# Feed-forward gate and up products as 2x2 block products with seven multiplications

## The chip, the cores and the metric

The kernel runs on one core of one Trainium2 chip. The metric is the device time of one execution in microseconds (us). A core has five engines that run side by side, each taking its own instructions in program order: TensorE (PE in the profile) multiplies matrices into PSUM banks of 128 x 512 floats, VectorE (DVE), ScalarE (ACT) and GpSimd (POOL) work elementwise, and SyncE (SP) issues most of the loads. Engines wait for one another by semaphores; DMA transfers run beside all of them.

## What is computed

The reference is a trunk of two layers over 512 tokens of 1024 features. Each layer is: half a feed-forward, a mixer (attention, and in the second layer a short convolution beside it), cross attention to 256 memory tokens, and half a second feed-forward. The part that the change touches runs four times:

```python
def rms_norm(x, g):
    y = xf * lax.rsqrt(jnp.mean(xf * xf, axis=-1, keepdims=True) + RMS_EPS)
    return (y * g).astype(x.dtype)

def swiglu(h, w_in, w_out):                     # D_MODEL 1024, D_FF 2816
    g, u = split_cols(h @ w_in, (D_FF, D_FF))
    return (jax.nn.silu(g) * u) @ w_out

x = x + 0.5 * swiglu(rms_norm(x, g[0]), ffn1_w_in[layer], ffn1_w_out[layer])
```

## The kernel before

**Layout and precision.** The residual `x` lies transposed in SBUF, eight tiles `x0` to `x7` of 128 features x 512 tokens. Every dense product is done in three: each operand is held as a high part (its rounding to the matmul's reduced float format) and a low part (the remainder), and `mm3` (line 321) issues high x high, high x low and low x high into one bank. The class `Norm` keeps the two parts of x times gain as `xh0..7` and `xl0..7`, and the sums of squares; the factor of each token is not multiplied in but applied to the product's result, by a row `rrow` of 512 factors (`row_ev` says that it is there).

**Weights.** They stream through the class `Weights`: a chunk of 128 x 1024 floats is loaded by SP into one of three `raw` buffers, ACT rounds it into `wh`, DVE subtracts to get `wl` (three buffers of each). Tokens stand for buffers: `tok_raw`, `tok_w` and so on; who gets a token may use a buffer.

**The feed-forward.** `ffn` (line 641) takes the 22 tiles of 128 hidden features in three parts, `PARTS` (7, 7 and 8). For each tile j it makes the gate product and the up product with `proj_t` (line 521): weights stationary, eight k-tiles, three matmuls of 512 columns each, 24 matmuls for a product and 48 for the pair. `gate` and `up` evacuate the banks with `rrow`, apply Silu, multiply, and split the result into `gated`, high and low. After a part, `out_proj` (line 591) multiplies its tiles into the eight feature tiles of x, one PSUM bank after the other, and adds them with DVE. In the last part its end (`done`) feeds the next stage's `Norm`. In the very first feed-forward the first pair runs as `pair_t`, two products side by side as the input comes.

**The order of the work.** Every engine takes its instructions in the order in which they are traced. That order is made by the class `Sched` (line 123): the kernel is written as tasks (generators) which yield what they wait for; the planner prices every instruction as it is traced (`price`, line 163), and of the tasks that can go on at the planned time of the tensor engine, the most urgent goes on. Priority 0 is the most urgent; the spine, which issues the products, has 5. `splitter` holds a chunk back until the planned queues of ACT and DVE are shorter than half a microsecond, unless the chunk is among the next two. `setup` (line 965) loads the small parameters and makes the rotation tables and the norm of the memory, during the first feed-forward.

**Buffers.** Nine slots of 8 KB per partition (`tok_slot`) hold gated tiles, heads of the attention and so on. PSUM has three banks "m", two "s" and two for transposes, one "o".

## Time and profile before

| | |
|---|---|
| time, median of 3 runs | 2279.39 us (2278.57 to 2280.5) |
| span of the profiled execution, first to last instruction | 2277.6 us |
| granted TensorE clock, mean | 0.999 |
| HBM traffic | 217.34 MB read, 4.21 MB written |
| DMA, mean over the span | 97 GB/s |

The page gives the profiled execution by its span; no separate time of it is listed. The runs were made without a profile.

How to read the lines: a group names the source line (all are L103 here, since one helper records every operation), the engine, the operation, then output tile <- input tiles, the shape, how often, busy time, mean time of one in ns, and the engine's idle time before these with what ended it. PEld is the weight load of TensorE, which overlaps its matmuls. The duration of a matmul overlaps the next one, so the rate is read from the distance of their starts. The chain in order of time lists start, length and what ended last, with the number of instructions merged. A row of windows gives the stretch, its length, the busy time (and number of instructions) of PE, PEld, DVE, ACT and POOL, then the granted clock, the DMA share and GB/s.

### The profile page before, as it was taken

What the parts mean: (1) busy time and instruction counts of PE and PEld (TensorE: products, weight loads), DVE (VectorE), ACT (ScalarE), POOL (GpSimd) and SP (SyncE); (2) the same over time, 40 slices, a digit from 0 to 9 for tenths busy, and PEclk for the clock granted to TensorE, in tenths of its full rate; (3) what the DMA queues carried; (4) which work ended last, traced back from release to release, by engine and by line L of the source; (5) the groups of instructions that cost most, each with busy time, mean ns of one, the idle gap of its engine ahead of it and who ended that gap; (6) DMA issues with size and microseconds to landing.
All of it is one profiled execution on the core that took longest, in us unless ns stands there. A gap on an engine that the chain in (4) does not pass through costs nothing.

```text
span 2277.6 us, 28369 instructions
## 1 busy us (share of the span) xinstructions
PE 2261.4 (99%) x11324; PEld 1899.0 (83%) x11324; DVE 1195.6 (52%) x1811; ACT 864.3 (38%) x1373; POOL 251.1 (11%) x288
## 2 busy tenths in 40 slices
PE   9999999999999999999999999999999999999999
PEld 7888888889888888888888888889888888888887
DVE  6444445576676654444454444455766666434443
ACT  6222234556555442222332222335544554323231
POOL 2100003432220010000010000023122001000000
PEclk9999999999999999999999999999999999999999
DMA  5432322212332232323232323333123332232332
GB/s 169 141 102 93 102 88 90 65 57 78 118 105 90 93 93 93 102 93 102 87 106 87 106 88 104 98 112 97 61 91 114 106 98 92 88 106 89 102 98 84
DMA packets 67509, 221.32 MB, mean 97 GB/s; under 512 B 9464, under 2 KB 11512, under 8 KB 67376
## 3 DMA queue, kind: packets, MB, share of 16 engines
q1 hardware_dynamic: 63936, 214.01, 29.9%
q0 software_dynamic: 3440, 5.49, 0.8%
q8 instruction: 89, 1.46, 0.2%
q14 instruction: 44, 0.36, 0.1%
HBM read 217.34 MB, written 4.21 MB: 97 GB/s over the span
## 4 chain that ended last, share of the span: by engine, by line
PE 90%; issue 3%; DVE 3%; POOL 3%; ACT 1%; DMA 0%; SPq 0%; POOLq 0%; DVEq 0%; ACTq 0%
PE ps_m L103 56%; PE ps_o L103 27%; PE ps_pv L103 2%; PE ps_s L103 1%; PE ps_x L103 1%; PE xo L103 1%; POOL qe L103 1%; PE ps_pt L103 1%; POOL qrr L103 1%; DVE wl L103 1%; DVE xl L103 1%; POOL rp L103 1%; DVE x L103 0%; PE ss L103 0%; PE qt L103 0%
## 5 line engine op out<-in xcount | busy, mean ns | idle before, releaser
L103 ACT ACTIVATE wh<-raw 128x1024 fp32r<-128x1024 f32 (+3 forms) x403 | 416.5, 1037 | 1064.8 <-PE ps_m L103 597.7
L103 PE MATMUL ps_m<-xh,wh 128*128 128x512 f32 x1640 | 643.3, 392 | 1.5 <-ACT wh L103 1.5
L103 PE MATMUL ps_m<-xh,wl 128*128 128x512 f32 x1640 | 639.5, 390 | 0.0
L103 PE MATMUL ps_m<-xl,wh 128*128 128x512 f32 x1640 | 639.1, 390 | 0.0
L103 DVE TENSOR_TENSOR wl<-raw,wh 128x1024 fp32r<-128x1024 f32 (+3 forms) x403 | 482.1, 1199 | 97.4 <-ACT wh L103 94.8
L103 PE MATMUL ps_o<-gated,wh 128*128 128x512 f32 x1408 | 433.4, 389 | 0.0
L103 PEld LDWEIGHTS ps_m<-xh,wh 128*128 128x128 f32 x1640 | 307.5, 188 | 66.6 <-ACT wh L103 2.0
L103 PEld LDWEIGHTS ps_m<-xh,wl 128*128 128x128 f32 x1640 | 307.4, 187 | 66.4 <-DVE wl L103 1.0
L103 PEld LDWEIGHTS ps_m<-xl,wh 128*128 128x128 f32 x1640 | 307.5, 188 | 62.7
L103 PEld LDWEIGHTS ps_o<-gated,wh 128*128 128x128 f32 x1408 | 264.3, 188 | 54.8
L103 PE MATMUL ps_o<-gated,wl 128*128 128x512 f32 x704 | 273.9, 389 | 0.0
L103 DVE SCALAR_TENSOR_TENSOR x<-ps_o,x 128x512 f32<-128x512 f32 x160 | 109.8, 690 | 286.5 <-PE ps_o L103 285.8
L103 DVE TENSOR_TENSOR us<-ps_m,rrow 128x512 f32<-128x512 f32 x88 | 60.9, 692 | 281.1 <-PE ps_m L103 281.1
L103 POOL TENSOR_TENSOR acc<-acc,sq 128x512 f32<-128x512 f32 x42 | 71.9, 1712 | 1056.8 <-ACT sq L103 1052.6
L103 PE MATMUL ps_m<-wh,xh 128*128 128x256 f32 x576 | 169.6, 295 | 0.0
L103 PE MATMUL ps_m<-wh,xl 128*128 128x256 f32 x576 | 162.7, 282 | 0.0
L103 PE MATMUL ps_m<-wl,xh 128*128 128x256 f32 x576 | 162.7, 282 | 0.0
L103 DVE TENSOR_TENSOR gs<-ps_m,rrow 128x512 f32<-128x512 f32 x88 | 60.9, 692 | 192.9 <-PE ps_m L103 189.8
L103 PEld LDWEIGHTS ps_o<-gated,wl 128*128 128x128 f32 x704 | 132.1, 188 | 27.6
L103 PEld LDWEIGHTS ps_m<-wh,xh 128*128 128x128 f32 x576 | 110.1, 191 | 1.8 <-issue 1.2
L103 PEld LDWEIGHTS ps_m<-wl,xh 128*128 128x128 f32 x576 | 110.2, 191 | 0.1
L103 PEld LDWEIGHTS ps_m<-wh,xl 128*128 128x128 f32 x576 | 109.9, 191 | 0.0
(228 smaller groups left out, 2287.7 us busy)
## 6 DMA issues: line engine op xcount, KB each, us to landing
raw<-ffn_in SPq DMA_DIRECT2D x174, 512.0 KB, 3.5
raw<-ffn_oa SPq DMA_DIRECT2D x64, 448.0 KB, 3.3
raw<-ffn_ob SPq DMA_DIRECT2D x32, 512.0 KB, 3.5
raw<-x_kv SPq DMA_DIRECT2D x32, 512.0 KB, 3.5
raw<-even_w SPq DMA_DIRECT2D x24, 512.0 KB, 3.5
raw<-x_q SPq DMA_DIRECT2D x16, 512.0 KB, 3.5
raw<-odd_w SPq DMA_DIRECT2D x12, 512.0 KB, 3.5
raw<-odd_wc SPq DMA_DIRECT2D x12, 512.0 KB, 3.6
```

The lines of the kernel that those rows point to most:

```text
L103: r = fn(*args, **kw)
```

## The change

From the 4th tile of each feed-forward on (`FILL = 3`), gate and up of a tile are no longer two products of 24 matmuls. The 1024 input features are cut in two halves of four k-tiles, the 512 tokens in two halves of 256 (`HS`); gate and up rows are the other way of halving. The 2 x 2 blocks of weights A and of input B are multiplied with seven block products in place of eight (Winograd's form of Strassen's method). Each block product is four k-tiles of three matmuls with 256 columns.

The sums of input blocks are made once a feed-forward by `Norm.seven` after `rrow` is there: for each of four k-tile pairs x gain x row for both tiles, four additions, and seven operands of 256 columns split in high and low parts. They lie in seven slots, with an eighth as scratch; the gated tiles move into the `xh`/`xl` tiles that are no longer needed.

The sums of weight blocks are made for each pair. The load of `s31` brings A11 and A22, an accumulating DMA from GpSimd's queue adds A21 to both; GpSimd then adds `s2` and `s4`. Five operands are split by ACT and DVE for a pair: `a1` (A11 and A12) and `s31`, 1024 columns each, `a22`, `s2`, `s4`, 512 each. The buffers of `wh` and `wl` become six of one kind.

`Pair` runs the products so that one bank, `b1`, gathers partial sums; after some products ACT copies it (`c1`, `c2`, `c3`) before the next product is added. The last two products of a pair (`p4`, `p3`) run within the next pair, and those of the last pair of a part within the first output product. The input parts `xh4..7` of the next stage wait until the last output product has read the gated tiles there. `setup` starts after the last round of `seven`. The planner's price of a matmul rises from n / 2400 to (n + 32) / 2400.

```diff
+FILL = 3
+HS = S // 2
...
-                cost = n / 2400.0 if n >= 256 else 0.213
+                cost = (n + 32) / 2400.0 if n >= 256 else 0.213
...
+        def loads(self):
+            h = WMAX // 2
+            yield tok_p
+            t = tp.tile([P, WMAX], F32, tag="P", name="s31")
...
+            sync.dma_start(out=t2, in_=bass.AP(self.w1.tensor, self.w1.offset,
+                                               [list(self.w1.ap[0]), [gap, 2], [1, h]]))
+            sch.add(self.acc(t, t2), 2)
+            yield W.tok_raw
+            self.a1.load()
+            yield tok_a22
+            u = tp.tile([P, h], F32, tag="ph", name="a22")
+            sync.dma_start(out=u, in_=self.w2[:, h:])
...
+        def acc(self, t, t2):
+            yield Need([t])
+            a21 = self.w2[:, :WMAX // 2].unsqueeze(1).to_broadcast([P, 2, WMAX // 2])
+            swdge.dma_start(out=t2, in_=a21, accum_op=ALU.add)
...
+        def add(self):
...
+            pool.tensor_tensor(s2, t[:, h:], a1[:, :h], ALU.add)
...
+            pool.tensor_tensor(s4, s2, a1[:, h:], ALU.add)
...
+        def seven(self):
+            yield self.row_ev
+            yield tok_slot
+            t = slot([8, HS], "hn", F32)
+            for kk in range(4):
...
+                for j in range(2):
+                    d = kk + 4 * j
+                    dve.scalar_tensor_tensor(
+                        out=t[:, 2 * j:2 * j + 2, :].rearrange("p a c -> p (a c)"), in0=x[d],
+                        scalar=gains[:, self.idx * KD + d:self.idx * KD + d + 1], in1=self.row,
+                        op0=ALU.mult, op1=ALU.mult)
+                dve.tensor_tensor(t[:, self.NT1], t[:, self.B11], t[:, 1], ALU.subtract)
+                dve.tensor_tensor(t[:, self.T3], t[:, self.B22], t[:, 1], ALU.subtract)
+                for o, u, v in ((self.NT2, self.T3, self.B11), (self.T4, self.NT2, self.B21)):
+                    dve.scalar_tensor_tensor(out=t[:, o], in0=t[:, u], scalar=-1.0, in1=t[:, v],
+                                             op0=ALU.mult, op1=ALU.subtract)
+                yield Need([t])
+                for r, src in runs:
+                    act.activation(r[:, :, 0, :], src, AF.Copy)
+                yield Need([r[:, :, 0, :] for r, _ in runs])
+                for r, src in runs:
+                    dve.tensor_tensor(r[:, :, 1, :], src, f(r[:, :, 0, :]), ALU.subtract)
+                self.bev[kk].set()
...
+        def product(self, ps, w, op, start):
+            for kk in range(4):
+                yield self.nrm.bev[kk]
+                c = slice(kk * P, (kk + 1) * P)
+                bh, bl = self.nrm.operand(op, kk)
+                yield Need([bl, w[1][:, c]])
+                mm3(ps[:, :HS], w[0][:, c], w[1][:, c], bh, bl, start and kk == 0, kk == 3, not start)
...
+        sch.add(nrm.seven(), 3)
...
+                g = Pair(nrm, res)
+                yield from g.p1_p2()
+                if last:
+                    yield from last.p4()
+                yield from g.p6()
+                if last:
+                    yield from last.p3()
+                yield from g.p5_p7()
+                last = g
...
-            yield from out_proj(list(range(j0, j1)), 1, gated, 0.5, done if pi == 2 else None, True)
+            yield from out_proj(list(range(j0, j1)), 1, gated, 0.5, done_, True,
+                                (last.p4(), last.p3()), read)
...
-        sch.add(setup(nrm.row_ev), 4)
+        sch.add(setup(nrm.bev[3]), 4)
```

## The prediction

> **What bounds the kernel now.** First the page: its span, its busy rows, its chain.

> ```profile
> span 2277.6 us, 28369 instructions
> PE 2261.4 (99%) x11324; PEld 1899.0 (83%) x11324; DVE 1195.6 (52%) x1811; ACT 864.3 (38%) x1373; POOL 251.1 (11%) x288
> ...
> PE 90%; issue 3%; DVE 3%; POOL 3%; ACT 1%; DMA 0%; SPq 0%; POOLq 0%; DVEq 0%; ACTq 0%
> ```

> The chain that ended last is matmul for nine tenths. A busy share of 99% alone would prove little, as matmul ends are modelled; so next the chain in order of time, over the second feed-forward.

> ```profile
> 815.34 69.39 PE ps_m L103 x306
> 884.73 38.08 PE ps_o L103 x168
> 922.81 76.16 PE ps_m L103 x336
> 998.97 38.08 PE ps_o L103 x168
> 1037.05 87.04 PE ps_m L103 x384
> ```

> Each piece begins where the one before ends: nothing waits, TensorE alone sets the pace. 76.16 / 336 = 0.2267 us is the pitch of a 512-column matmul. A gate/up pair is 2 x 8 x 3 = 48 of them, 10.88 us. The median of the runs shown, 2279.39 us, is 1.8 us above this span; I sum against the span and add 1.8 at the end.

> **What is removed.** Four feed-forwards have 22 pairs each; three of each stay as they are, so 4 x 19 = 76 pairs change. A changed pair has 7 products of 4 k-tiles x 3 = 84 matmuls of 256 columns. The mixer already issues that width with a weight load for each, in the timeline:

> ```profile
> 399.78 0.28 PE L103 MATMUL ps_m<-wh,xh 128*128 128x256 f32 x1
> ...
> 405.78 0.28 PE L103 MATMUL ps_m<-wh,xl 128*128 128x256 f32 x1
> ```

> These are 50 starts apart: 6.00 / 50 = 0.120 us. So 84 x 0.120 = 10.08 us stands for 10.88: 0.80 us a pair, **76 x 0.80 = 60.8 us** in all. One eighth of the arithmetic goes, but only 7.4% of the time, since 0.120 is more than half of 0.2267.

> [...]

> **What is added in each changed pair, beside the matmuls.** Unit prices, from the groups with shapes kept apart, and in the last row from the view of the tile `acc` (shortest, median, longest in ns):

> ```profile
> L103 DVE TENSOR_TENSOR wl<-raw,wh 128x1024 fp32r<-128x1024 f32 x334 | 409.6, 1228 | 93.6 <-ACT wh L103 93.5
> L103 ACT ACTIVATE wh<-raw 128x1024 fp32r<-128x1024 f32 x334 | 353.5, 1060 | 832.3 <-PE ps_m L103 511.6 <-PE ps_o L103 171.8 <-issue 143.2
> L103 DVE TENSOR_TENSOR gated<-gs,gated 128x512 fp32r<-128x512 f32 x88 | 60.8, 691 | 0.0
> L103 ACT ACTIVATE gated<-gs 128x512 fp32r<-128x512 f32 x88 | 55.7, 633 | 54.8 <-DVE gs L103 54.8
> L103 DVE SCALAR_TENSOR_TENSOR v<-ps_m,rcol,v 128x256 fp32r<-128x256 f32 x24 | 10.5, 479 | 2.5 <-ACT v L103 2.4
> L103 ACT ACTIVATE v<-ps_m,rcol 128x256 fp32r<-128x256 f32 x24 | 10.0, 468 | 4.2 <-PE ps_m L103 4.1
> L103 POOL TENSOR_TENSOR acc<-acc,sq x42: 1287/1794/2059, 341.3 to 1914.2; 128x512 f32<-128x512 f32 x42
> ```

> Weight splits become two of 1024 columns and three of 512. DVE: 2 x 1.228 + 3 x 0.69, five 256-column combinations at 0.48, one low part at 0.69: 7.6 us of 10.08. ACT: 2 x 1.06 + 3 x 0.63, three copies at 0.47, Silu and high part 1.26: 6.7 us. POOL: two sums at 1.29 to 2.06 us, 4.1 at most, and the issue of one DMA. All lie beside the 10.08 us of matmuls, so I cost them at nothing; TensorE hides them.

> The cover is thinnest for the copies of b1, each between two products on one bank. In a steady pair two products (2.88 us) lie between, against about 0.47 for the copy, 0.28 for the last matmul's end and under 0.2 of hand-over: about 1 us. Up to 1.9 us of other ACT work may stand ahead, and the longest single piece is 1.06. In the first changed pair of a part there is no older pair to interleave, and only one product (1.44 us) lies between, twice: a 1.06 us split ahead would cost 0.6. 12 such parts at 0.4 us: **+5 us** (0 to 14).

> **The weight sums' chain.** The s31 load is issued from SP; behind it wait a1 and a22, and the down-projection's chunks. The accumulating DMA waits on POOL's queue for it; behind it stand the additions s2 and s4, on which ACT's splits wait, and behind those the copies. Nearest rows, of the DMA view (KB each, us from issue to landing; the last is a queue's packets, MB and share):

> ```profile
> raw<-ffn_in SPq DMA_DIRECT2D x174, 512.0 KB, 3.5
> rel_d<-rel POOLq DMA_DIRECT2D x2, 1024.0 KB, 16.5
> rel<-rel_d POOLq DMA_DIRECT2D x8, 256.0 KB, 3.8
> ...
> q1 hardware_dynamic: 63936, 214.01, 29.9%
> ```

> No accumulating transfer is in this trace. Its 512 KB lie between 3.5 us (plain, same size) and 16.5; the nearest row by shape is 256 KB from POOL in 3.8, so I take about 6. Two buffers alternate, so load 3.5 + transfer 6 + two additions at 1.8 each + a split's 2.3 = 15.4 must fit in two pairs, 20.2. It fits, at nothing; above about 11 it no longer does. Traffic goes from 1 to 1.75 MB a pair where the loads' queue has a share of 29.9% today: 30% x 1.75 is about half, not the bound.

> **What lands on the path: the operand sums.** Each feed-forward must first make 28 combined operands of its input (`seven`), in four rounds that share one buffer. A round: on DVE two 512-column products at 0.69 and four 256-column ops at 0.45, 3.2 us; on ACT 1792 columns at the 1024 row's rate, 1.9; on DVE 1792 again, 2.15; hand-overs 0.2. About 7.4 us, of which DVE 5.3. They start when `rrow` is there, and the fourth pair needs the last round. From the timeline of ACT, and a window of the second feed-forward:

> ```profile
> 25.37 0.60 ACT L103 ACTIVATE rrow<-rb 128x512 f32<-128x512 f32 x1 [3.88 <-PE rb L103]
> 815.38 0.60 ACT L103 ACTIVATE rrow<-rb 128x512 f32<-128x512 f32 x1 [0.97 <-PE rb L103]
> ...
> 815.98:841.18 25.20, 25.20 (x113) 20.86 (x112) 10.77 (x13) 8.59 (x11) 0.00 (x0) 1.00 0.35 104
> ```

> At 815.34, 336 - 306 = 30 matmuls of the part were done; the 144 of three pairs end 114 x 0.2267 later, at 841.18. The fourth pair's first product runs on rounds as they come and needs the last at 841.18 + 9 x 0.12 = 842.3. From 815.98 to there are 26.3 us. In that window DVE is already busy 10.8 us. Adding four rounds, 21.3: 32.1 us, so 848.1, a stall of 5.8 us if DVE never waits. Four rounds alone, unhindered, take 29.6: a stall of 3.3 is the least. If none of ACT's rounds were covered, 8 more than the sum: 13.8. I take 7, close to the DVE sum, since the fill pairs' own DVE work covers most of ACT's turns.

> The two other later feed-forwards start the same way, with 306 left (its rows 1175.33 and 1921.36); the first one does not. The chain in order of time again:

> ```profile
> 25.33 53.76 PE ps_m L103 x237
> ...
> 79.31 8.19 PE ps_m L103 x36
> ...
> 326.86 43.52 PE ps_o L103 x192
> ...
> 1175.33 69.39 PE ps_m L103 x306
> ...
> 1921.36 69.39 PE ps_m L103 x306
> ```

> There 237 + 36 = 273 were left at 25.33, 63 done already, so three pairs end 81 x 0.2267 later, at 43.7, and the last round is due at 44.8. It starts at 26.0: 26.0 + 32.1 = 58.1, a stall of 13.3; I take 14 (11 to 22). **3 x 7 + 14 = +35 us** (21 to 63).

> **The clock after a stall.** Two windows near the start, where the loads are awaited:

> ```profile
> 5.05:8.46 3.41, 1.91 (x8) 0.91 (x7) 1.66 (x4) 2.69 (x5) 0.00 (x0) 1.00 0.95 318
> 8.46:11.88 3.42, 3.42 (x9) 2.33 (x8) 3.42 (x6) 3.42 (x8) 0.00 (x0) 0.50 1.05 403
> ```

> After a stretch with TensorE busy 1.91 of 3.41 us the next 3.41 were granted 0.50. Four stalls of 7 to 14 us are as empty. Half a clock for at most 3.4 us costs at most 1.7: 4 x 0.8 = **+3 us** (0 to 7).

> [...]

> **Moved.** `setup` begins after the operand sums, no longer right behind `rrow` at 26.0 us; its POOL DMAs and additions then share POOL's queue with the accumulating DMAs of the first feed-forward. Its results are needed by the mixer, after the first feed-forward's last product at 326.86 + 43.52 = 370.4 us: nothing. The input parts 4 to 7 of the next stage wait until the last output product has read the buffers; four splits (DVE 4 x 0.69) in that product's 5.4 us: nothing, at worst 1 us in three places. The matmul price in the ordering changes the mixers' order, which I leave at zero, within 3 us either way.

> **Sum.** 2277.6 - 60.8 + 5 + 35 + 3 = 2259.8; with 1.8 outside the span, **2261 us**. Its own range is 2240 to 2282: the bounds of the start stalls, the parts and the clock.

> **Rivals.** (1) *The sums are hidden.* Should the order let `seven` run ahead of the fill pairs' evacuations, with ACT's and DVE's halves overlapping, the stalls and clock term go: 2277.6 - 60.8 + 5 + 1.8 = 2224. Against: DVE's 32 us do not fit in 26, nor even the lone rounds. For: durations overlap by some 0.08 us each, and evacuations can wait, as three banks are there. 0.16.

> (2) *Slower: the accumulating DMA sets the pace.* The two-buffer loop has 9.4 us beside it; it exceeds a pair's 10.08 us once the transfer passes 10.8. At 16.5 a pair takes 25.9 / 2 = 12.95 us, 2.9 over 10.08: 76 x 2.9 = 218 on top, 2479. The forecast gains 2279.4 - 2261 = 18 us; that is gone at 10.08 + 18 / 76 = 10.32 us a pair, a transfer of 11.2. For: the row of 16.5 is a POOL transfer. Against: it goes DRAM to DRAM, the rows into the chip's memory take under 4. 0.10.

> (3) *The copies come late in each pair*: ACT's and DVE's queues are strict, and a split that waits for POOL holds the copies behind it. 18 / 76 = 0.24 us lost a pair takes the gain; 0.5 us gives 2299. Against: 66% and 75% load, 1.9 us of room. 0.12.

> (4) *The change does not do what it says*: weights stationary with 256 moving columns cost more than 10.88 / 84 = 0.1295 us each. At 0.135, 84 x 0.135 - 10.88 = +0.46 a pair: 76 x 0.46 = 35 lost in place of 60.8 gained, so 2277.6 + 35 + 43 (the other terms) + 1.8 = 2357. Against: 0.120 held for 50 in a row. 0.02.

> **Chances.** The forecast has 0.60. Measurement can tell about 0.2%, 4.6 us, from no change: 2274.8 to 2284.0. The forecast's upper part gives 0.05 of its 0.60 to "same", rival 3 another 0.02, and rivals 2, 3, 4 the rest to slower: 0.10 + 0.10 + 0.02. Faster is 0.55 + 0.16 = 0.71. So 0.71, 0.07, 0.22. The range must take in (1) and the near part of (3): 2222 to 2295.

> **What would show it.** TensorE should have 11324 + 76 x 36 = 14060 matmuls; a stretch of steady pairs 10.08 us each with no idle between; at each feed-forward's fourth pair a gap of about 7 us (14 in the first) ended by the DVE low part of an operand tile, then half clock; ACT's and DVE's busy time in steady pairs near 66% and 75%. Wrong would be: gaps ended by copies inside steady pairs (3), splits ended by POOL or DMA with the landing above 11 us (2), or no gap at the fourth pair (1).

## The result, and the profile after

The changed kernel takes **2306.2 us** (median of 4 runs, 2304.4 to 2311.2) where the kernel before takes 2279.1 beside it: 1.0121 times, 95% interval 1.0107 to 1.0136. It is 27 us slower; 18 us faster was forecast. Times of runs here and below are medians; one execution in experiment 12, of 6565.5 us where its three others took 2245.5 to 2248.8, is left out. First the page of the kernel after: span, busy times, chain by engine.

```profile
span 2305.2 us, 35767 instructions
PE 2224.7 (97%) x14060; PEld 1993.9 (86%) x14060; DVE 1462.9 (63%) x2327; ACT 1086.7 (47%) x1869; POOL 569.1 (25%) x516
...
PE 77%; DVE 9%; issue 4%; POOL 4%; DMA 3%; ACT 3%; SPq 0%; POOLq 0%; ACTq 0%; DVEq 0%
```

The 14060 matmuls are those foreseen, and TensorE's busy time fell from 2261.4 to 2224.7 us; but its share of the chain fell from 90 to 77%, and 9% now belong to VectorE. TensorE has less to do and waits more. The page doesn't say where. So both traces are cut at landmarks (the start of the last output matmul of each stage), and the stages are compared:

| stage | before, us | after, us | difference |
|---|---|---|---|
| first feed-forward | 370.0 | 382.5 | +12.5 |
| first mixer | 296.3 | 313.5 | +17.2 |
| cross attention | 139.9 | 140.5 | +0.6 |
| second and third feed-forward | 721.0 | 716.4 | -4.6 |
| second mixer | 233.7 | 238.9 | +5.2 |
| cross attention | 151.3 | 150.7 | -0.6 |
| fourth feed-forward, and the end | 365.3 | 362.6 | -2.7 |

This table finds the surprise: **22.4 us of the loss lie in the two mixers, whose products the change doesn't touch.** The four feed-forwards together lose 5 us where 18 were to be gained. The rest of this section is about them; the chain in order of time, second feed-forward, shows what goes right and what wrong:

```profile
845.63 15.01 PE ps_m L106 x66
...
862.44 2.07 DVE bop L106 x3
864.51 1.67 DVE hn L106 x3
...
871.28 4.22 DVE bop L106 x3
875.50 1.67 DVE hn L106 x3
...
881.60 0.88 DVE bop L106
882.52 38.55 PE ps_m L106 x302
...
962.07 67.67 PE ps_m L106 x564
```

The last row is the gain: 67.67 / 564 = 0.120 us a matmul, as forecast, without a break. From 860 to 882 the chain leaves TensorE and runs along VectorE, through the low parts of the operands (`bop`) and their products and sums (`hn`). TensorE's timeline shows the two gaps in it, the first ended by ScalarE's high part of an operand, which had waited for VectorE's sums, the second by VectorE's low part:

```profile
878.55 0.58 PE L106 MATMUL ps_m<-bop,w 128*128 128x256 f32 x1 [5.98 <-ACT bop L106]
882.52 1.86 PE L106 MATMUL ps_m<-bop,w 128*128 128x256 f32 x7 [3.39 <-DVE bop L106]
```

Windows of the same kernel: the rounds, the clock's windows around them, and steady pairs (columns as before: stretch, length, busy PE, PEld, DVE, ACT, POOL, then clock, DMA share, GB/s).

```profile
846.30:882.50 36.20, 26.85 (x122) 22.02 (x120) 35.20 (x50) 16.80 (x22) 8.86 (x6) 0.92 0.38 92
...
876.95:887.19 10.24, 5.25 (x23) 4.96 (x24) 8.32 (x13) 4.49 (x6) 1.21 (x1) 0.50 0.35 104
887.19:897.43 10.24, 10.24 (x87) 10.24 (x87) 5.81 (x9) 5.01 (x9) 2.58 (x2) 1.00 0.44 93
...
1080.00:1140.00 60.00, 60.00 (x502) 60.00 (x502) 44.00 (x63) 33.79 (x58) 24.61 (x17) 1.00 0.68 178
```

While the four rounds run, VectorE is busy 35.2 of 36.2 us: it is the bound, as the prediction had it, but it was to need 32.1. From 876.95 on the clock is halved for 10.24 us. In steady pairs TensorE never rests, and VectorE at 73% and ScalarE at 56% (75 and 66 were forecast) have room. Why the rounds take longer is in the timeline of VectorE (start, length, instruction, how many):

```profile
855.51 3.48 DVE L106 SCALAR_TENSOR_TENSOR hn<-x,gains,rrow 128x512 f32<-128x512 f32 x2
862.36 2.15 DVE L106 TENSOR_TENSOR bop<-hn,bop 128x256 fp32r<-128x256 f32 x3
864.43 1.41 DVE L106 SCALAR_TENSOR_TENSOR hn<-x,gains,rrow 128x512 f32<-128x512 f32 x2
871.20 4.30 DVE L106 TENSOR_TENSOR bop<-hn,bop 128x512 fp32r<-128x512 f32 x3
```

and in GpSimd's, of the same kernel:

```profile
855.33 3.11 POOL L106 TENSOR_TENSOR s<-s,raw 128x512 f32<-128x512 f32 x2 [8.07 <-DMA s<-ffn_in]
871.43 3.79 POOL L106 TENSOR_TENSOR s<-s,raw 128x512 f32<-128x512 f32 x2 [11.83 <-DVE w L106]
```

The same two products take 1.41 us alone and 3.48 beside GpSimd's additions of weight blocks; the same three low parts 2.15 and 4.30. Both long ones lie in time on an addition: 2.07 + 2.15 = 4.2 us added in one feed-forward.

### The profile page after: what moved, and what is told of

The parts are those of the page before. It is cut to its first block, busy times and chain, and to the rows that moved or that the text cites. A ratio compares the mean times of both kernels' runs of the same rounds, so it can differ in the third digit from the quotient of the medians.

```text
span 2305.2 us, 35767 instructions
## 1 busy us (share of the span) xinstructions
PE 2224.7 (97%) x14060; PEld 1993.9 (86%) x14060; DVE 1462.9 (63%) x2327; ACT 1086.7 (47%) x1869; POOL 569.1 (25%) x516
## 4 chain that ended last, share of the span: by engine, by line
PE 77%; DVE 9%; issue 4%; POOL 4%; DMA 3%; ACT 3%; SPq 0%; POOLq 0%; ACTq 0%; DVEq 0%
PE ps_m L106 46%; PE ps_o L106 24%; DMA s<-ffn_in 2%; DVE w L106 2%; DVE bop L106 2%; POOL qrr L106 1%; PE ps_pv L106 1%; DVE hn L106 1%; POOL qe L106 1%; ACT w L106 1%; PE ps_s L106 1%; DVE xl L106 1%; PE ps_x L106 1%; PE xo L106 1%; PE ps_pt L106 1%
## 5 line engine op out<-in xcount | busy, mean ns | idle before, releaser
L106 PE MATMUL ps_m<-bop,w 128*128 128x256 f32 x6384 | 787.0, 286 | 48.1 <-ACT bop L106 27.5
L106 PEld LDWEIGHTS ps_m<-bop,w 128*128 128x128 f32 x6384 | 781.7, 194 | 54.8 <-ACT bop L106 28.6
L106 ACT ACTIVATE w<-raw 128x1024 fp32r<-128x1024 f32 (+2 forms) x327 | 335.0, 1028 | 426.5 <-PE ps_o L106 240.2
L106 DVE TENSOR_TENSOR w<-raw,w 128x1024 fp32r<-128x1024 f32 (+2 forms) x327 | 396.1, 1211 | 153.9 <-ACT w L106 145.3
L106 POOL TENSOR_TENSOR s<-s,raw 128x512 f32<-128x512 f32 x152 | 231.2, 1521 | 438.8 <-DMA s<-ffn_in 270.0
L106 PE MATMUL ps_o<-gh,w 128*128 128x512 f32 x1024 | 328.1, 389 | 0.0
L106 PE MATMUL ps_m<-xh,w 128*128 128x512 f32 (+1 forms) x848 | 278.4, 396 | 1.2 <-ACT w L106 1.2
L106 DVE TENSOR_TENSOR w<-s,w 128x512 fp32r<-128x512 f32 (+1 forms) x228 | 219.1, 961 | 71.4 <-ACT w L106 47.4
L106 PE MATMUL ps_m<-w,xh 128*128 128x256 f32 x1152 | 218.9, 289 | 0.0
L106 PE MATMUL ps_o<-gl,w 128*128 128x512 f32 x512 | 199.4, 389 | 0.0
## 6 DMA issues: line engine op xcount, KB each, us to landing
raw<-ffn_in SPq DMA_DIRECT2D x98, 512.0 KB, 4.8
s<-ffn_in SPq DMA_DIRECT2D x76, 512.0 KB, 4.3
s<-ffn_in POOLq DMA_DIRECT2D x76, 512.0 KB, 5.9
a<-ffn_in SPq DMA_DIRECT2D x76, 256.0 KB, 3.8
raw<-ffn_ob SPq DMA_DIRECT2D x32, 512.0 KB, 3.5
raw<-x_kv SPq DMA_DIRECT2D x32, 512.0 KB, 3.5
raw<-even_w SPq DMA_DIRECT2D x24, 512.0 KB, 3.4
```

Source lines behind the costliest of these rows:

```text
L106: r = fn(*args, **kw)
```

## The experiments

Theories at the start. For the mixers: **A**, the planner's new matmul price makes the order worse; against it, **B**, something else of the change (buffers, moved set-up work) costs there. For the feed-forwards: the rounds of operand sums, the set-up work, and the clock, each with its own price. Below, "stage" numbers are differences from the kernel before, in us, by the landmarks above; each comes from one profiled execution. That of experiment 2 is the slowest of its ten (2284.2 us, the median is 2281.5), so stage numbers measured against it can be some 3 us too large in sum.

**1. The price alone, in the kernel before.** One line, nothing of the products changed:

```diff
-                cost = n / 2400.0 if n >= 256 else 0.213
+                cost = (n + 32) / 2400.0 if n >= 256 else 0.213
```

> The kernel before with one line of the change: the planner prices a matmul at (n + 32) / 2400. Nothing of the seven products. In the changed kernel's trace the first mixer is 17.2 us longer and the second 5.2. Theory A, the price alone reorders the mixers for the worse: 2279 + 22 = 2301 us, all of it in the two mixers. Rival, the mixers are late because of what was moved into them or of shared buffers: within 3 us of 2279.

Measured: 2298.7, ratio 1.0087 [1.0072, 1.0102]; first mixer +13.4, second +4.7, feed-forwards 0. A window over the first mixer of the kernel before:

```profile
370.00:667.00 297.00, 292.06 (x2101) 258.19 (x2100) 198.47 (x391) 170.93 (x355) 98.21 (x118) 1.00 0.27 84
```

and over that of this kernel, 13 us longer as its mixer is:

```profile
370.00:680.00 310.00, 295.64 (x2099) 258.46 (x2097) 198.92 (x391) 171.45 (x354) 94.71 (x118) 1.00 0.27 81
```

Nearly the same instructions, the same VectorE and ScalarE time, the same clock; TensorE's idle time went from 297.00 - 292.06 = 4.9 to 14.4 us; the other 3.6 are longer matmul times, whose ends are modelled. A number that no engine sees, only the planner, costs 19.6 us.

**2. The change with the old price.** The same line set back in the changed kernel.

> The changed kernel with the old price of n / 2400. Theory A: the mixers come back to 296 and 234 us, 2306 - 22 = 2284 us; the feed-forwards may shift by some us, as their order is made by the same price. Rival (moved work or buffers): mixers stay long, 2306 within 4.

Measured: 2281.5, ratio 1.0009 [1.0000, 1.0019], 24.7 below the changed kernel; mixers -0.1 and +0.4, first feed-forward +14.2, the others -3.3, -3.0, -3.0. Undoing the price restores both mixers: A is right, B falls. What is left of the change is then even with the kernel before.

**3. Half the price step, in the kernel before** (n + 16).

> The kernel before with a price of (n + 16) / 2400, half way. If the mixers lose steadily with the price, because a lower price of matmuls makes the planner put more of them into each wait of a chain: about half of 19.5, 2289 us. Rival, the order is simply another one and its luck another: anywhere from 2275 to 2305, not between the two.

Measured: 2287.0, ratio 1.0032 [1.0020, 1.0044]; mixers +6.9 and +1.6. 0, +7.6, +19.6 us for 0, 16, 32: the loss grows at both steps, which speaks against one unlucky order; three orders don't make a rule.

**4. Other prices raised along with it.** If the old price was good only because the other engines are priced too low as well, longer planned hand-overs should win the loss back:

```diff
-    LAG = {"pe": 0.2, "act": 0.15, "dve": 0.14, "pool": 0.08, "dma": 2.0, "swdge": 2.2}
+    LAG = {"pe": 0.2, "act": 0.2, "dve": 0.19, "pool": 0.13, "dma": 2.0, "swdge": 2.2}
...
+                cost = (n + 32) / 2400.0 if n >= 256 else 0.213
```

> The kernel before with the new price of (n + 32) / 2400 and 0.05 us more of planned hand-over after ACT, DVE and POOL instructions. Theory: the old, too low price had stood in for hand-overs that the planner takes too short; with longer hand-overs and the true price the mixers come back: 2280 to 2285. Rival, the hand-overs aren't what is short: 2299 within 4.

Measured: 2292.8, ratio 1.0059 [1.0042, 1.0076]: 6 of the 20 us come back, less than the theory asked and more than the rival allowed. The balance of prices is a part of it; the rest isn't explained.

**5. One round of operand sums in place of four**, the price as in the change. The other three k-tile pairs use the operands of the first, so three quarters of the input sums aren't computed.

```diff
-            for kk in range(4):
+            for kk in range(1):
...
-                self.bev[kk].set()
+                for ev in self.bev:
+                    ev.set()
```

> The changed kernel with one of the four rounds of operand sums; the other three k-tile pairs use the first round's operands, so that part of the input isn't computed. Theory: the idle stretches of TensorE at the fourth pair (10.2 us in three feed-forwards, some 16 in the first) and the half clock behind them (about 3 us each, 7 in the first) are the price of the rounds: about 2306 - 46 - 16 = 2244 us, and the granted clock stays at 1.0 after the start. Rival, the fourth pair waits for its weight sums (accumulating DMA, POOL) and not for the rounds: no more than 15 us better, 2291 or above, with gaps at the same place.

Measured: 2259.1, ratio 0.9916 [0.9901, 0.9931]. The three later feed-forwards stand at -14.5, -13.4, -14.5, near the 19 x 0.80 = 15.2 that the arithmetic is worth: there the rounds, with the half clock that follows them, are nearly the whole loss. The run still misses the theory's 2244 by 15 us, and the first feed-forward shows where: it stands at +2.6, some 17 above its sisters, without the rounds. TensorE rests there for 7.5 us from 45.57 on. Rows of ScalarE's and TensorE's timelines (`u` is ScalarE's copy of the bank `b1`):

```profile
50.92 0.23 ACT L106 ACTIVATE cos_t<-rr 128x32 f32<-128x32 f32 x1 [1.06 <-DVE rr L106]
...
52.38 0.23 ACT L106 ACTIVATE sin_t<-rr 128x32 f32<-128x32 f32 x1 [0.97 <-DVE rr L106]
52.64 0.23 ACT L106 ACTIVATE sin_t<-sin_t 128x32 f32<-128x32 f32 x1
52.78 0.36 ACT L106 ACTIVATE u<-ps_m 128x256 f32<-128x256 f32 x1
...
53.20 3.15 PE L106 MATMUL ps_m<-bop,w 128*128 128x256 f32 x13 [7.35 <-ACT u L106]
```

`setup` makes the rotation tables with some twenty short VectorE instructions, one after the other, and ScalarE waits for them before its own part. The copy stands behind that part in ScalarE's queue, though the product that it copies was done by 45.9. GpSimd's weight addition, behind nine loads of `setup` on its queue, was over by 47.8 and is not what ended the gap. In the kernel before, the same instructions stand in ScalarE's queue from 39.11 to 45.57 and TensorE's chain runs on unbroken: plain pairs have no such copy between their matmuls.

**6. Four fill pairs in place of three**, the price as in the change. The fourth plain pair's gated tile needs a slot, which it gets when the rounds are done; `setup` starts then.

> The changed kernel with four unchanged pairs ahead in place of three: the rounds have 10.88 us more, at 0.8 us a feed-forward. If VectorE is what the rounds wait for, the added pair brings it 4.8 us of work as well, so a stall shrinks by 6 of its 10 us, to about 4, and the half clock behind it by a part: 2306 - 4 x 6 - 8 + 3 = 2277 us. Rival, the rounds are bound by their own serial hand-overs: the whole 10.2 us are covered, three stalls vanish and the first shrinks to 6: 2306 - 41 - 13 + 3 = 2255 us.

Measured: 2289.3, ratio 1.0048 [1.0033, 1.0063], 12 above the theory. In the later feed-forwards the two gaps became one of 2.9 us, and the stages stand at -9.2, -7.7, -9.2; in the first, where `setup` again moved, the gaps only changed places (+15.2). The longest, of 5.9 us, is now at a matmul of `setup` itself, which waits in TensorE's queue for GpSimd's sums of the memory's squares:

```profile
205.03 0.69 PE L106 MATMUL ss<-ident,setup 128*128 128x128 f32 x2 [5.73 <-POOL setup L106]
```

Cover in front of the rounds works; the first feed-forward's trouble is another.

**7. GpSimd's additions out of the way**: old price, and for the first two changed pairs of each feed-forward GpSimd writes zeros in place of the sums `s2` and `s4`, so these sums aren't computed.

```diff
-            pool.tensor_tensor(s2, t[:, h:], a1[:, :h], ALU.add)
+            if self.blank:
+                pool.memset(s2, 0.0)
```

> The changed kernel with the old price (2281.5 us) where GpSimd, for the first two changed pairs of each feed-forward, writes zeros in place of adding s2 and s4: those two sums are left out there. Theory: GpSimd's additions lengthen VectorE's work in the rounds (3.48 us for two products that take 1.41 elsewhere, 4.30 for low parts that take 2.15), so the last round comes some 4 us sooner and each of the three later stalls shrinks from 9 to 5: 2281.5 - 12 = 2269, a little less with a shorter half clock. Rival, the rounds are long by VectorE's own work alone: within 3 us of 2281.5.

Measured: 2266.7, ratio 0.9944 [0.9929, 0.9959], 14.9 below experiment 2. Three pieces of VectorE's timeline in experiment 2, a round's low parts, the next one's products and a weight split, each while GpSimd adds (from 836.50 for 4.04 us and from 859.91 for 3.78):

```profile
836.21 3.18 DVE L106 TENSOR_TENSOR bop<-hn,bop 128x1024 fp32r<-128x1024 f32 x2
839.31 2.44 DVE L106 SCALAR_TENSOR_TENSOR hn<-x,gains,rrow 128x512 f32<-128x512 f32 x2
...
860.29 2.28 DVE L106 TENSOR_TENSOR w<-s,w 128x1024 fp32r<-128x1024 f32 x1
```

and the same three in this kernel, where GpSimd writes zeros instead (from 852.11 for 0.98 us beside the split):

```profile
830.62 2.09 DVE L106 TENSOR_TENSOR bop<-hn,bop 128x1024 fp32r<-128x1024 f32 x2
832.63 1.41 DVE L106 SCALAR_TENSOR_TENSOR hn<-x,gains,rrow 128x512 f32<-128x512 f32 x2
...
852.56 1.21 DVE L106 TENSOR_TENSOR w<-s,w 128x1024 fp32r<-128x1024 f32 x1
```

1.1 + 1.0 + 1.1 us of VectorE time are gone, and the gaps of the later feed-forwards go from 3.0 + 5.9 to 0.9 + 4.5 us: 3.5 less, for 3.2 of VectorE time. So the stretching lands on the path. The first feed-forward gains too, from +14.2 to +8.6. (The zeros are also written sooner than sums, so splits may wait less; that isn't parted from it.)

**8. TensorE kept busy in the gap**, old price: a task of the lowest priority issues matmuls whose results nobody uses, until the last round is ordered.

> The changed kernel with the old price (2281.5 us) and, while the fourth pair waits for the rounds, matmuls whose result nobody reads, on a free bank, so that TensorE isn't idle there. The stalls stay as they are. Theory: the half clock (10.24 us in each later feed-forward, 17 in the first) comes from the idle time; it stays at 1.0 now and the matmuls that ran at half clock give back 8 us: 2273. Rival, the matmuls at half clock only eat slack that the weights' splits need anyway: within 2 us of 2281.5.

Measured: 2282.0, ratio 1.0012 [1.0003, 1.0022]. A gap of 6.0 us stayed in each later feed-forward, and the clock still fell for 10.24 us there, so nothing follows from these about the clock. In the first, the half-clock windows shrank from 17.07 us to two of 3.41 and the stage went from +14.2 to +10.7 in the trace; the median shows no gain.

**9. The same until the planner expects the last low part:**

```diff
+        while not nrm.bev[3].on or sch.when(nrm.operand(6, 3)[1]) > sch.t["pe"] - 1.0:
+            mm(ps, nrm.hi[7][:, :P], nrm.hi[7], True, True)
```

> As the run before with idle-time matmuls (2282.0 us), where they stopped once the last round had been ordered, so that a stretch of 6.0 us stayed empty and the clock fell all the same. Here they go on until the planner expects the last low part to be there. Theory: the granted clock stays at 1.0 in the three later feed-forwards, their matmuls at half clock (some 20 each at 0.213 in place of 0.120 us) give back 2 us each and the first feed-forward's 3 more: 2281.5 - 8 = 2273. Rival, the time lost at half clock hides behind the splits: within 2 us of 2281.5.

Measured: 2282.1, ratio 1.0019 [1.0009, 1.0028], no gain over experiment 2. Yet the half-clock windows of the later feed-forwards shrank from 10.24 to 3.41 us. The chain in order of time behind the stall, in experiment 2:

```profile
865.17 34.87 PE ps_m L106 x266
```

and in this one:

```profile
864.80 37.78 PE ps_m L106 x302
```

Against 0.120 us a matmul, that is 34.87 - 31.92 = 2.95 us too long, and 37.78 - 36.24 = 1.54: 1.4 less in a feed-forward. The stages show 0.7, 0.4 and 1.7 less. So in the traces the clock costs about what the count says, but 3 us in all are no more than the scatter of these runs (2280.8 to 2288.4), and the medians don't confirm it.

**10. The first feed-forward left as before**, old price: its 22 pairs are plain, `setup` begins at `row_ev` again, the other three are as changed.

```diff
+    def fills(kind, layer):
+        return NF if kind == "ffn1" and layer == 0 else FILL
...
-        sch.add(setup(nrm.bev[3]), 4)
+        sch.add(setup(nrm.row_ev), 4)
```

> The changed kernel with the old price where the first feed-forward keeps its eight block products and setup starts where it did before; the other three are changed. Theory: the first feed-forward loses 14 us to its stall, its half clock and to setup's instructions and DMAs on GpSimd's queue between the weight sums; without them it is back at 370: 2281.5 - 14 = 2267. Rival, moving setup harms only later: first feed-forward at 370 but the first mixer longer by as much, 2280.

Measured: 2272.0, ratio 0.9969 [0.9957, 0.9981]. The first feed-forward is back at 0.0 (from +14.2), the others at -4.2, -1.1, -2.9; by the medians the run gains 9.5 us on experiment 2. This shows that the change loses there; it takes rounds and moved `setup` out together and doesn't part them.

**11. The same with five fill pairs** (`FILL = 5`) in the other three; the two late tiles share a slot taken after the rounds.

> As the run with an unchanged first feed-forward, but with five unchanged pairs ahead in the three changed ones. One pair more took a stall from 10.2 to 3.0 us; two more should cover it wholly: each changed feed-forward at 361 - 17 x 0.8 + 0.5 = 348 us, 2279 - 39 = 2240, granted clock 1.0 throughout. Rival, VectorE, loaded 75% in steady pairs, passes the lateness on, and a stall of 3 us stays: 2252.

Measured: **2244.1, ratio 0.9845 [0.9830, 0.9860]**, the fastest of all, 35 us below the kernel before. Its page:

```profile
span 2240.9 us, 33297 instructions
PE 2223.3 (99%) x13160; PEld 1954.0 (87%) x13160; DVE 1377.7 (61%) x2168; ACT 1015.8 (45%) x1709; POOL 464.5 (21%) x441
...
PE 89%; DVE 4%; POOL 2%; issue 2%; ACT 1%; DMA 1%; SPq 0%; POOLq 0%; DVEq 0%; ACTq 0%
```

and a window over the rounds of its second feed-forward:

```profile
815.23:880.29 65.06, 65.06 (x355) 56.73 (x355) 53.38 (x79) 32.65 (x47) 8.48 (x6) 1.00 0.41 118
```

TensorE doesn't rest, the clock stays full; VectorE is busy 53.4 of the 65.1 us, so the rounds now fit beside the fill pairs. The three feed-forwards stand at -12.4, -11.8, -12.4, of 17 x 0.80 = 13.6 to be had.

**12. The same with a price below the old one** (n - 16).

> The run with an unchanged first feed-forward and five unchanged pairs ahead (2244 us), with a price still lower, (n - 16) / 2400. If the mixers' loss simply falls with the price (19.5 us at +32, 7.6 at +16, 0 at 0), some 3 us more are to be had: mixers at 293 and 232, 2240. Rival, the planner's hand-overs suit a price near n / 2400 and the loss rises on both sides: 2244 to 2252.

Measured: 2246.2 (median of three), ratio 0.986 [0.984, 0.988]; mixers +2.0 and -0.3, the first cross attention +2.5. The loss doesn't go on falling below the old price.

## Why the prediction was wrong

The miss is 45 us. Half of it, 22.4 us, is a term of the sum that had been set to nothing, the planner's price in the mixers. The other half is in the feed-forwards: the stalls 10.3 us and the clock 7.9 us too small, and `setup` at nothing. Either half alone is as large as the gain of 18 that was forecast: with the old price (experiment 2) the changed kernel is still 2.4 us slower than the kernel before, not faster. Step by step:

**What is removed: right.** 84 matmuls at 0.120 us; the chain gives 0.120 and the pairs have no idle time (502 matmuls in 60 us). Experiment 5 brings 13.4 to 14.5 of the 15.2 in a later feed-forward, so the 60.8 stand.

**Work beside the matmuls and accumulating DMA: right; copies: right in size by luck.** Two rows of the DMA view of the kernel after (KB, median us to landing):

```profile
s<-ffn_in SPq DMA_DIRECT2D x76, 512.0 KB, 4.3
s<-ffn_in POOLq DMA_DIRECT2D x76, 512.0 KB, 5.9
```

5.9 us where 6 was taken, and the longest transfer took 10.7; rivals 2 and 4 fall. So does rival 3 for the steady pairs: the waits of 0.16 to 0.71 us between matmuls of block products are 14 and sum to 4.4 us. That is near the +5 for the parts' first pairs, but seven of the 14 come just before, between or right behind the long stalls, and the largest, 0.71 us, lies near the end of the first feed-forward; the first pairs of second and third parts show none above 0.13.

**"DVE 5.3" a round, and "I take 7" and "14": right in mechanism, too small.** The gaps came at the fourth pair, ended by the operands' parts, the last by VectorE's low part. By distances of starts less 0.12 they are 6.1 + 3.9 = 10.0 us in the second feed-forward, 9.7 and 10.0 in the next two, and 6.3 + 3.8 + 4.0 + 1.5 = 15.6 in the first. The prediction had summed VectorE's own instructions at their lone durations, 32.1 us; GpSimd's additions put 4.2 on top, and experiment 7 shows that they do it. "About 7" with a bound of 13.8 held the value; the total of 35 became 45.3. The sum's own range was added up wrongly: its bounds (0 to 14, 21 to 63, 0 to 7) give 2240 to 2303 us, not 2240 to 2282.

**Moved, "its results are needed by the mixer ...: nothing": wrong.** The step asked when `setup`'s results are needed, not what stands behind its instructions. It named GpSimd's queue; the gaps go through ScalarE's. In the kernel after, a further gap of 3.4 us in the first feed-forward (at 72.57) ends as the 7.5 us of experiment 5 do, with the copy behind the rotation tables:

```profile
75.52 0.23 ACT L106 ACTIVATE sin_t<-sin_t 128x32 f32<-128x32 f32 x1
75.66 0.37 ACT L106 ACTIVATE u<-ps_m 128x256 f32<-128x256 f32 x1
...
76.08 1.22 PE L106 MATMUL ps_m<-bop,w 128*128 128x256 f32 x4 [3.23 <-ACT u L106]
```

That is rival 3's mechanism, a copy held back in ScalarE's queue, with `setup` in place of a split. How `setup` and rounds share the first feed-forward's loss was not parted: leaving it as before saves 14.2 us in the traces, 9.5 by the medians (experiment 10).

**The clock, "+3 (0 to 7)": too small.** The step took one window of 3.41 us at half clock. At each of the later stalls it is 10.24, in the first feed-forward 17.07 and 6.83. 116 matmuls of block products are about 0.09 us late, 10.9 us in all. That is a count in the trace; the direct test (experiment 9) has the right sign in its trace, but no median shows the cost. In the second feed-forward TensorE's idle gaps were 6.0 and 3.4 us. Half clock came with shorter ones too: 2.9 us of idle time in experiment 6 was followed by 3.41 us of it, and in the first of the prediction's two windows, ahead of 3.42 us at 0.50, TensorE's longest gap is 1.07 us.

**"The matmul price in the ordering ... I leave at zero, within 3 us either way": this is the step that failed most.** The mixers lose 22.4 us; the price alone costs the kernel before 19.6, and undoing it gives the kernel after 24.7 back. The bound of 3 us was worked out from nothing: no row of the profile before gives it, so both ends should have been wide, and a rival should have carried it. The new price, moreover, is the truer one: (256 + 32) / 2400 = 0.120 and (512 + 32) / 2400 = 0.2267 are the measured pitches. A truer price gave a worse order; experiment 4 recovers a third of the loss by raising other prices, and why the rest stays is open.

**The account.** 2277.6 - 60.8 + 45.3 (rounds) + 3.4 (the gap at `setup`) + 4.4 (parts) + 10.9 (clock) + 22.4 (mixers) = 2303.2, against a span of 2305.2. Of the 2 us left, 1.4 are a gap at 106.71 in the first feed-forward, where ScalarE's queue waits for one of `setup`'s loads of the memory. The clock's 10.9 are the count above.

**Rival 1** (sums hidden) doesn't hold for three fill pairs. Experiment 11 does hide them in three feed-forwards, but by more cover in front, not by the order that the rival named.

## What to carry to other kernels

Where a kernel's order comes from a planner, a changed price is a change to every stage: try it by itself, and don't price it at nothing because no instruction moves on paper. For preparation work that must be done before faster work can start, sum the bound engine's time with what its neighbours do to it, and put enough other work in front: here two more plain pairs gave up 1.6 us of gain a feed-forward and removed 8.9 us of stall and the half clock behind it (experiments 10 and 11). For a moved task, ask what stands behind its instructions on each engine's queue as well as when its results are needed: the same set-up work cost nothing among plain pairs and stopped TensorE among pairs that need a copy in between.

## What the runs showed of the hardware

**GpSimd's additions lengthened VectorE's instructions.** Two VectorE products went from 1.41 to 3.48, three low parts from 2.15 to 4.30 and a weight split from 1.21 to 2.28 us beside GpSimd's additions of weight blocks. Beside GpSimd writing zeros (experiment 7), for 0.5 us of its length, the split stayed at 1.21.
